# Two transformer blocks on one core: the experts' weights in loads of 2 MB, the last sums onto x, and a branch's loads on another queue

## Chip, core and metric

The kernel runs on one core of a Trainium2 chip. The metric is the device time of one execution in microseconds. PE is the matrix engine, PEld its weight loads, DVE, ACT and POOL (GpSimd) the vector, scalar and general engines, SP the engine whose queue issues nearly all DMAs.

## Reference

256 tokens of width 1024 in float32 go through two blocks. Block 1 has one layer: a mixer (attention over selected keys beside a state-space mixer), then 32 experts of which each token takes 4. Block 2 has two layers of dilated attention beside mLSTM and a convolutional feed-forward part.

```python
def first_block(x, c, ...):
    mod = cond @ w_ada + b_ada
    h = _rms(x, norm_mix) * (1.0 + sc_m) + sh_m
    ...
    x = x + g_m * (mixed @ w_out)
    h = _rms(x, norm_ffn) * (1.0 + sc_f) + sh_f
    x = x + g_f * _moe(h, w_router, b_router, w_gu, b_gu, w_dn, b_dn)

def second_block(x, ...):
    for l in range(2):
        mixed = hybrid_mixer(rms_norm(x, mix_pre_g[l]), w_in[l], ...)
        x = x + rms_norm(mixed, mix_post_g[l])
        ff = conv_ffn(rms_norm(x, ffn_pre_g[l]), w_up[l], ...)
        x = x + rms_norm(ff, ffn_post_g[l])
```

`_moe` takes the top 4 of 32 router values per token, their softmax as gates, and sums `gate * (swiglu(h @ w_gu[e] + b_gu[e]) @ w_dn[e] + b_dn[e])`. `w_gu[e]` is 1024 x 2048 (8 MB), `w_dn[e]` 1024 x 1024 (4 MB).

## The kernel before, in words

All tokens stay in SBUF. The program runs through three stages. The mixer of block 1 ends at about 340 us of the profiled span, the experts at about 1290, and the two layers of block 2 fill the rest.

**The experts.** `moe` gives each expert 64 slots of tokens. `Expert.gate_up(j)` (L1410) takes piece j of `w_gu`, 128 rows of 2048 values: 1 MB, 8 KB a partition. It has four matmul calls, pg and pu (gate and up), each on two halves of the array (64 rows of the output each). `Expert.turn` prepares the way back to tokens, `act` the swiglu (sw_g, sw_t, sw_u) and its transposes (pat), `down` (L1457) multiplies by `w_dn` in four loads of 1 MB into pdn. `out` scales (oe), splits it in two parts (oeH, oeL), and `scatter` (L1487) adds it onto x with two matmuls (pc) and one DVE add for each half of each of two token blocks. In `moe` (L1352) the next expert's piece 0 is multiplied before the expert's `down`, and the sums onto x of an expert stand among the next one's pieces. `in_order` with `TEN` keeps PE's instructions in the written order.

**The ring.** `k.load` puts each weight load into the next of 20 slots of 1 MB (`ring_use`: pools that lie where the mixer's buffers were, in the order `RU`). The loads are on SP's queue; a load is issued when the slot's last reader is done.

**The block past the slots.** Ahead of expert 18, `overflow` (L1506) stands in an `If` (L1512) on the largest count of tokens of an expert. It is not executed with these inputs. Its own loads are on SP's queue too.

**The last expert.** Its sums onto x are also squared on ACT (sq_y) for the next norm (rn_m, rs, then xs on DVE and nf_p, the transposes on PE). `k.warm` puts small matmuls (warm) between, whose result is not used. `OL` sets the order of the norm's steps.

Some lines that matter:

```python
w = k.load([(lambda t: t, self.w_gu[e, j * 128:(j + 1) * 128, :])], [128, 2048])
for n, (p, o) in enumerate(outs):
    nc.tensor.matmul(p[o:o + 64], hg, w[:, n * 512:(n + 1) * 512], ...)
...
with tc.If(go > SLOTS):
```

Of the kernel before, what the change touches and what calls it, by code (L numbers as in the profile page):

```python
# [8 lines left out]
F32 = mybir.dt.float32  # L9
# [4 lines left out]
OP = mybir.AluOpType  # L14
# [12 lines left out]
SD = 1  # L27
OL = 'r0 r1 t00 t01 H00 L00 H01 L01 t10 H10 t11 L10 H11 L11'
# [71 lines left out]
def _pack(a):  # L100
# [13 lines left out]
    for k in ("norm_mix", "b_ada", "norm_ffn", "conv_w", "conv_b", "ssm_norm", "kv_norm"):  # L114
        col(k, a[k])
    col("d_skip", np.repeat(np.asarray(a["d_skip"]).reshape(-1), 64))
# [11 lines left out]
    return {"vec": vec, "row": row.reshape(1, NR)}  # L128

# [16 lines left out]
class K:  # L146
    def __init__(self, tc, i, ctx):
# [13 lines left out]
        self.hold = []  # L161
        self.side = 0
# [53 lines left out]
    def late(self, P):  # L216
# [7 lines left out]
        nc.sync.dma_start(self.wro, i["w_router"][0].rearrange("(k p) e -> p k e", p=128))  # L224
# [79 lines left out]
    def split(self, w, eng=None, into=None):  # L304
# [19 lines left out]
        with ExitStack() as c:  # L324
            for inst in self.hold.pop(0) if self.hold else ():
                c.enter_context(self.tc.issue_after(inst))
            self.splits = [self.nc.scalar.activation(H, w, AF.Copy).ins,  # L327
                           (eng or self.nc.vector).tensor_tensor(L, w, H.bitcast(F32), op=OP.subtract).ins]  # L328
        return H, L
# [159 lines left out]
def ada_end(k, n, s, ones):  # L489

    nc = k.nc
    o = k.ps.tile([128, 512], F32, name="ad_c", tag="tr", bufs=2)
    for j in range(4):
        k.lastc = nc.tensor.matmul(o[:, j:j + 1], s[:, j * 128:(j + 1) * 128], ones, start=True, stop=True)
    kind, half = n // 2, n % 2
# [45 lines left out]
def mixer(k):  # L541
# [185 lines left out]
    def scores(b):  # L727
        S = 128 * (b + 1)
        acc = sm.tile([128, 256], F32, name="acc", bufs=1)[:, :S]
        for g in range(4):  # L730
            h0 = (g // 2) * 4 + g % 2
            pd = ps.tile([128, 2, 256], F32, name="pd", tag="at", bufs=2)
            for u in range(2):
                h = h0 + 2 * u
                o = (h % 2) * 64
                nc.tensor.matmul(pd[:, u, :S], qiT[o:o + 64, h // 2, b * 128:(b + 1) * 128], kiT[o:o + 64, :S],
                                 start=True, stop=True)
            rl = sm.tile([128, 2, 256], F32, name="rl", tag="t2", bufs=3)
            nc.scalar.activation(rl[:, :, :S], pd[:, :, :S], AF.Relu)
            for u in range(2):  # L740
                h = h0 + 2 * u
                if g == 0 and u == 0:
                    nc.vector.tensor_scalar(acc, rl[:, u, :S], wi[:, b, h:h + 1], 0.0, op0=OP.mult, op1=OP.add)
                else:
                    nc.vector.scalar_tensor_tensor(acc, rl[:, u, :S], wi[:, b, h:h + 1], acc,
                                                   op0=OP.mult, op1=OP.add)
# [62 lines left out]
    def attend(q):  # L809
        PT0 = Bp.tile([128, 4, 256], F32, name="PT0", tag="PT0")  # L810
        PT1 = Bp.tile([128, 4, 128], F32, name="PT1", tag="PT1")
        for b in range(NB):
# [3 lines left out]
            for u0 in range(2):  # L816
                pl = ps.tile([128, 2, 256], F32, name="pl", tag="at", bufs=2)
                for u in range(2):
# [3 lines left out]
                                     kT[o:o + 64, h // 2, :S], start=u == 0, stop=False, skip_group_check=True)  # L822
                nc.tensor.matmul(pl[:, :, :S], identr, msk[b][:, None, :].to_broadcast([128, 2, S]),
# [21 lines left out]
        for g in range(2):  # L845
            p = ps.tile([128, 256], F32, name="pv", tag="at", bufs=2)
            for u in range(2):
                hs = slice((4 * q + 2 * g + u) * 64, (4 * q + 2 * g + u) * 64 + 64)
                o = p[u * 64:u * 64 + 64]
                nc.tensor.matmul(o, vv[:, 0, hs], PT0[:, 2 * g + u], start=True, stop=False)  # L850
                nc.tensor.matmul(o[:, 128:], vv[:, 1, hs], PT1[:, 2 * g + u], start=False, stop=True)
# [115 lines left out]
    def quad(q):  # L967
# [17 lines left out]
        for w in range(2):  # L985
            j = 2 * q + w
            p = ps.tile([128, 256], F32, name="py", tag="at", bufs=2)
            for u in range(2):
                h = 2 * j + u
                o = p[u * 64:u * 64 + 64]  # L990
                hs = slice(h * 64, h * 64 + 64)
                nc.tensor.matmul(o, xdt[:, 0, hs], wm[:, 0:2, 2 * w + u], start=True, stop=False)
                nc.tensor.matmul(o[:, 128:], xdt[:, 1, hs], wm[:, 2, 2 * w + u], start=False, stop=True)
# [91 lines left out]
    def turn(b, j0, jn, psum, eng):  # L1085

        p = ps.tile([128, 4, 128], F32, name="xt_p", tag=psum, bufs=2)
        for j in range(jn):
            k.tr(p[:, j], k.x[:, b, (j0 + j) * 128:(j0 + j + 1) * 128])
# [1038 lines left out]
```

## Time and profile before

| | |
|---|---|
| median of 3 runs | 2036.26 us (2033.62 to 2036.63) |
| the profiled execution | 2033.31 us, of which the span is 2031.6 us |
| mean granted clock of PE | 0.975 |
| PE busy | 1889.1 us, 93% of the span |
| DVE, ACT, POOL busy | 1051.6, 746.0, 210.8 us |
| DMA | 583.21 MB in 188091 packets |

Shares of busy time are averages over the three stages. In the experts' stage the DMA rate is level; in the others it is less than half of that. The chain of waits tells which of them a step waits for, and a timeline row's bracket how long its engine was idle before it and what released it.

### The profile page before, as it was taken

The page shows a single profiled execution, that of the slowest core. Times are in us where ns is not written, and L with a number is a line of the kernel's source. Part 1 is how long each engine was busy: PE and PEld are TensorE (multiplying, and loading weights), DVE is VectorE, ACT ScalarE, POOL GpSimd, SP SyncE. Part 2 cuts the span into 40 slices and gives each one's busy share as a digit, 9 for nine tenths or more (in the row PEclk, how much of TensorE's full clock was granted, in tenths as well). Part 3 has the DMA queues.
Part 4 walks back from the last instruction along what each step waited for, and adds up shares of the span by engine and source line. Part 5 has one row for each costly group of instructions (what it writes and reads, how often), then busy time and mean ns, then how long its engine had stood idle before and what let it go on. Part 6 is the DMA issues. An engine that isn't in the chain of part 4 may idle for free.

```text
span 2031.6 us, 28326 instructions
## 1 busy us (share of the span) xinstructions
PE 1889.1 (93%) x11058; PEld 1217.5 (60%) x11059; DVE 1051.6 (52%) x1919; ACT 746.0 (37%) x1477; POOL 210.8 (10%) x378
## 2 busy tenths in 40 slices
PE   6799999999999998869999998898999999989998
PEld 5688887444344433324443333676799877769996
DVE  3788675223222222202222222388689758778984
ACT  4657444111011110101111110355577545556763
POOL 1434310000000000000000000111022111111210
PEclk9899999999999999979999999899999999999999
DMA  9767558999999999999999999633265545325552
GB/s 341 254 224 227 158 201 309 398 420 421 420 420 421 420 420 420 420 374 421 419 420 421 420 420 420 234 131 98 84 208 181 175 149 192 104 83 177 187 177 94
DMA packets 188091, 583.21 MB, mean 287 GB/s; under 512 B 15096, under 2 KB 92424, under 8 KB 138928
## 3 DMA queue, kind: packets, MB, share of 16 engines
q1 hardware_dynamic: 186960, 578.32, 74.3%
q0 software_dynamic: 704, 1.98, 0.4%
q8 instruction: 89, 1.46, 0.3%
q10 hardware_dynamic: 288, 1.05, 0.1%
q14 instruction: 50, 0.41, 0.1%
HBM read 580.23 MB, written 1.07 MB: 286 GB/s over the span
## 4 chain that ended last, share of the span: by engine, by line
PE 37%; DMA 9%; DVE 6%; issue 2%; ACT 1%; POOL 0%; DVEq 0%; POOLq 0%; ACTq 0%; SPq 0%
PE mm L340 8%; PE mm L341 8%; PE mm L339 8%; DMA w<-in_w_gu_dram 6%; DMA w<-in_w_dn_dram 3%; PE pdn L1465 3%; PE pg L1424 3%; PE pu L1424 2%; DVE wL L328 1%; DVE ac L1936 1%; PE apv L1917 1%; ACT wH L327 1%; PE warm L403 0%; PE apl L1895 0%; PE pc L1493 0%
## 5 line engine op out<-in xcount | busy, mean ns | idle before, releaser
L328 DVE TENSOR_TENSOR wL<-w,wH 128x1024 fp32r<-128x1024 f32 (+1 forms) x239 | 307.6, 1288 | 118.3 <-ACT wH L327 115.0
L327 ACT ACTIVATE wH<-w 128x1024 fp32r<-128x1024 f32 (+1 forms) x255 | 267.6, 1052 | 177.0 <-PE mm L340 81.0
L1424 PE MATMUL pg<-w,hg 128*64 128x512 f32 x1024 | 278.2, 616 | 27.4 <-DMA w<-in_w_gu_dram 21.5
L1424 PE MATMUL pu<-w,hg 128*64 128x512 f32 x1024 | 269.0, 597 | 0.0
L1465 PE MATMUL pdn<-w,aT 128*64 128x512 f32 x1024 | 228.4, 595 | 5.9 <-DMA w<-in_w_dn_dram 4.1
L341 PE MATMUL mm<-hnH,wL 128*128 128x256 f32 x800 | 229.1, 286 | 1.2 <-POOL xp L1931 0.8
L339 PE MATMUL mm<-hnH,wH 128*128 128x256 f32 x800 | 226.5, 283 | 0.0
L340 PE MATMUL mm<-hnL,wH 128*128 128x256 f32 x800 | 226.2, 283 | 0.0
L1162 ACT ACTIVATE sw_t<-sw_g 128x512 f32<-128x512 f32 x32 | 20.2, 630 | 466.3 <-DVE sw_g L1161 466.3
L1479 DVE SCALAR_TENSOR_TENSOR oe<-pdn,gs,gf 128x512 f32<-128x512 f32 x32 | 24.0, 751 | 316.6 <-PE pdn L1465 316.6
L1465 PEld LDWEIGHTS pdn<-w,aT 128*64 128x64 f32 x1024 | 72.4, 137 | 156.3 <-issue 122.2
L1424 PEld LDWEIGHTS pu<-w,hg 128*64 128x64 f32 x1024 | 75.3, 138 | 148.2 <-issue 148.2
L341 PEld LDWEIGHTS mm<-hnH,wL 128*128 128x128 f32 x800 | 153.2, 191 | 3.5 <-DVE wL L328 1.3
L339 PEld LDWEIGHTS mm<-hnH,wH 128*128 128x128 f32 x800 | 153.3, 192 | 0.5 <-issue 0.4
L1424 PEld LDWEIGHTS pg<-w,hg 128*64 128x64 f32 x1024 | 60.2, 137 | 155.7 <-issue 77.5
L340 PEld LDWEIGHTS mm<-hnL,wH 128*128 128x128 f32 x800 | 153.3, 192 | 0.0
L1496 DVE TENSOR_TENSOR x<-x,pc 128x512 f32<-128x512 f32 x128 | 82.4, 684 | 122.2 <-PE pc L1494 122.2
L1480 ACT ACTIVATE oeH<-oe 128x512 fp32r<-128x512 f32 x32 | 20.2, 630 | 277.9 <-DVE oe L1479 277.9
L341 PE MATMUL mm<-hH,wL 128*128 128x256 f32 x304 | 91.0, 299 | 11.3 <-DVE wL L328 11.3
L328 POOL TENSOR_TENSOR wHL<-w,wHL 128x1024 fp32r<-128x1024 f32 x1 | 2.4, 2359 | 938.0 <-DMA w<-in_w_in_dram 938.0
L2068 DVE SCALAR_TENSOR_TENSOR fa<-fx,lvec,fa 128x256 f32<-128x256 f32 x176 | 92.7, 527 | 5.1 <-ACT fa L2066 4.3
L339 PE MATMUL mm<-hH,wH 128*128 128x256 f32 x304 | 90.5, 298 | 4.8 <-ACT wH L327 4.3
(551 smaller groups left out, 3426.9 us busy)
## 6 DMA issues: line engine op xcount, KB each, us to landing
w<-in_w_gu_dram SPq DMA_DIRECT2D x256, 1024.0 KB, 19.8
w<-in_w_dn_dram SPq DMA_DIRECT2D x127, 1024.0 KB, 19.8
w<-in_w_in_dram SPq DMA_DIRECT2D x50, 1024.0 KB, 5.6
w<-in_w_up_dram SPq DMA_DIRECT2D x44, 1024.0 KB, 5.1
w<-in_w_down_dram SPq DMA_DIRECT2D x20, 1024.0 KB, 5.0
ad_l<-in_w_ada_dram SPq DMA_DIRECT2D x32, 512.0 KB, 4.3
w<-in_w_out_dram SPq DMA_DIRECT2D x12, 1024.0 KB, 5.1
w<-in_w_ada_dram SPq DMA_DIRECT2D x8, 1024.0 KB, 14.3
```

The costliest lines, as they stand in the source:

```text
L327: self.splits = [self.nc.scalar.activation(H, w, AF.Copy).ins, (eng or self.nc.vector).tensor_tensor(L, w, H.bitcast(F32), op=OP.subtract) ...
L328: (eng or self.nc.vector).tensor_tensor(L, w, H.bitcast(F32), op=OP.subtract).ins]
L339: nc.tensor.matmul(out, sH, mH, start=start, stop=False, **kw)
L340: nc.tensor.matmul(out, sH, mL, start=False, stop=False, **kw)
L341: return nc.tensor.matmul(out, sL, mH, start=False, stop=stop, **kw)
L1424: nc.tensor.matmul(p[o:o + 64], hg, w[:, n * 512:(n + 1) * 512], start=j == 0, stop=j == 7 and e > 0)
L1465: nc.tensor.matmul(pd[c * 64:c * 64 + 64], self.aT[:, j % 4, j // 4], w[:, j - j0, c * 512:(c + 1) * 512], start=j == 0, stop=j == 7)
L1479: nc.vector.scalar_tensor_tensor(oe, self.pd, self.gs, k.gf, op0=OP.mult, op1=OP.mult)
L1496: dx = nc.vector.tensor_tensor(xx, xx, p, op=OP.add)
L1917: nc.tensor.matmul(p[u * 64:u * 64 + 64], vv[:, sb, hs], PT[:, sb, 2 * g + u], start=sb == 0, stop=sb == 1)
L1936: nc.vector.scalar_tensor_tensor(ac, xp[:, q:q + 256], cw[:, q * 8 + j:q * 8 + j + 1], ac, op0=OP.mult, op1=OP.add)
L2068: nc.vector.scalar_tensor_tensor(ac, xp[:, q:q + 256], cw(q, j), ac, op0=OP.mult, op1=OP.add)
```

## The change

1. **Loads.** `w_gu` comes in four loads of 2 MB an expert, `w_dn` in two: a partition reads 16 KB in one run (two rows of `w_gu`, four of `w_dn`). So that the rows match, the features are taken in pairs (`pair(j)`: every second column), the norm's vectors are permuted where the program lays out its inputs, and `act` is transposed by every fourth column. The ring has 10 slots of 2 MB. `TEN` holds SP too, so loads go out in PE's order. The last expert's last pieces come in smaller loads.
2. **The block past the slots** has its loads on GpSimd's queue.
3. **The last sums onto x**: the warm matmuls stand behind all four sums; the four pc have four PSUM buffers; sq_y has another buffer; `behind` keeps the first square after the split of the second weight piece on ACT; `OL` is reordered.
4. **Half-array alternation**: pd, pl, pv, py (mixer of block 1) and apl, apv (block 2) are written so that calls on the two halves of the array take turns.

```diff
-OL = 'r0 r1 t00 t01 H00 L00 H01 L01 t10 H10 t11 L10 H11 L11'
+OL = 'r0 t00 t01 r1 H00 L00 H01 L01 t10 H10 t11 L10 H11 L11'
...
+def pair(j):
+    c = j // 2 * 256 + j % 2
+    return slice(c, c + 255, 2)
...
+    def ring_use(self, order):
+        self.rctx.close()
+        self.shared.close()
+        self.wctx.close()
+        self.big = ExitStack()
+        left, right = (NW + len(self.wz)) // 2, self.nring // 2
+        p = [(self.big.enter_context(self.tc.tile_pool(name=f"big{n}", bufs=1, side="left" if n < left else "right",
+                                                       reuse_waits="tile")), 1) for n in range(left + right)]
+        self.rings, self.nload = [p[n] for n in order], -1
...
-RU = (0,-3,1,2,-1,-2)
+RU = (4,5,3,6,0,1,2,7,8,9)
...
-TEN = (mybir.EngineType.PE,)
+TEN = (mybir.EngineType.PE, mybir.EngineType.SP)
...
-        w = k.load([(lambda t: t, self.w_gu[e, j * 128:(j + 1) * 128, :])], [128, 2048])
+        if j % 2 == 0:
+            src = self.w_gu[e, j * 128:j * 128 + 256, :].rearrange("(p k) c -> p k c", k=2)
+            parts = [slice(0, 1), slice(1, 2)] if self.final and j == 6 else [slice(0, 2)]
+            self.w = k.load([(lambda t, c=c: t[:, c], src[:, c]) for c in parts], [128, 2, 2048])
+        w = self.w[:, j % 2]
...
-            k.tr(pt[:, q].rearrange("p a s -> p (a s)"), act[:, c:c + 255:2])
+            k.tr(pt[:, q].rearrange("p a s -> p (a s)"), act[:, q:q + 509:4])
...
+        for a in range(2):
+            src = self.w_dn[e, a * 512:a * 512 + 512, :].rearrange("(p k) c -> p k c", k=4)
+            parts = [slice(0, 2), slice(2, 3), slice(3, 4)] if self.final and a else [slice(0, 4)]
+            w = k.load([(lambda t, c=c: t[:, c], src[:, c]) for c in parts], [128, 4, 1024])
+            for q in range(4):
                 for c in range(2):
...
+                if E[e].final:
+                    for b in range(NB):
+                        for c in range(2):
+                            k.warm(k.x[:, b, c * 512:c * 512 + 128], WE[3 + 2 * b + c])
...
                 if self.final:
-                    sq = self.M.tile([128, 512], F32, name="sq_y", tag="st", bufs=BST)
+                    sq = self.M.tile([128, 512], F32, name="sq_y", tag="sg", bufs=BSG)
                     aq = nc.scalar.activation(sq, xx, AF.Square, scale=1 / 32, accum_out=k.ssx[:, b, c:c + 1])
-                    k.warm(xx[:, :128], WE[3 + 2 * b + c])
+                    if b + c == 0:
+                        k.behind = aq.ins
...
-                            nc.sync.dma_start(w, w_gu[0, bass.ds(e, 1), j * 128:(j + 1) * 128, c0:c0 + 512]
+                            nc.gpsimd.dma_start(w, w_gu[0, bass.ds(e, 1), pair(j), c0:c0 + 512]
...
-            for u0 in range(2):
-                pl = ps.tile([128, 2, 256], F32, name="apl", tag="at", bufs=2)
-                for u in range(2):
+            pls = [ps.tile([128, 2, 256], F32, name="apl", tag="at", bufs=2) for u0 in range(2)]
+            for u in range(2):
+                for u0, pl in enumerate(pls):
                     h = 4 * q + u0 + 2 * u
                     o = (h % 2) * 64
                     nc.tensor.matmul(pl[:, u], qT[0][o:o + 64, h // 2, b * 128:(b + 1) * 128], qT[1][o:o + 64, h // 2],
                                      start=True, stop=True)
+            for u0, pl in enumerate(pls):
                 nc.vector.tensor_tensor(lg[:, u0:u0 + 3:2], pl, logc[:, b:b + 1].to_broadcast([128, 2, 256]), op=OP.add)
```

How the order of the instructions moves, at three places. First SP's queue where the experts start; a row is the line, the instruction and its tile (cmi is the largest count). Before:

```order
L301 DMA w<-in_w_gu_dram 128x2048 x3
L1301 DMA bgu_r<-in_b_gu_dram 128x512
L1303 DMA bdn<-in_b_dn_dram 32x512 x2
L301 DMA w<-in_w_gu_dram 128x2048 x3
L301 DMA w<-in_w_dn_dram 128x2048 x2
L1511 TENSOR_LOAD cmi
L1511 ISA x2
L301 DMA w<-in_w_dn_dram 128x2048 x2
L301 DMA w<-in_w_gu_dram 128x2048 x8
L301 DMA w<-in_w_dn_dram 128x2048 x4
L301 DMA w<-in_w_gu_dram 128x2048 x8
```

Now:

```order
L323 DMA w<-in_w_gu_dram 128x4096 x2
L1329 DMA bgu_r<-in_b_gu_dram 128x512
L1331 DMA bdn<-in_b_dn_dram 32x512 x2
L323 DMA w<-in_w_gu_dram 128x4096 x2
L1546 TENSOR_LOAD cmi
L1546 ISA x2
L323 DMA w<-in_w_dn_dram 128x4096 x2
L323 DMA w<-in_w_gu_dram 128x4096 x4
L323 DMA w<-in_w_dn_dram 128x4096 x2
L323 DMA w<-in_w_gu_dram 128x4096 x4
L323 DMA w<-in_w_dn_dram 128x4096 x2
L323 DMA w<-in_w_gu_dram 128x4096 x4
```

Loads of 16 KB a partition (4096 values) stand in for two of 8 KB, and expert 1's first piece goes out with its partner ahead of expert 0's `w_dn`, as PE reads it.

Second, SP at the branch ahead of expert 18, with the semaphores that each row waits for: DMAHW are the hardware DMA lanes (loads issued by SP), DMASW the software ones (GpSimd), `sequencer` the engine's own. The last row is the jump past the block. Before:

```order
L301 DMA w<-in_w_gu_dram 128x2048 [waits DMAHW0_49,PE_49]
L301 DMA w<-in_w_gu_dram 128x2048 [waits DMAHW1_49,PE_49]
L301 DMA w<-in_w_gu_dram 128x2048 [waits DMAHW2_49,PE_49]
L1512 COMPARE_AND_BRANCH
L1524 COMPARE_AND_BRANCH
L1524 UNCONDITIONAL_BRANCH [waits SP_sequencer_49,DMAHW0_49,DMAHW1_49,DMAHW2_49,DMAHW3_49,DMAHW4_49,DMAHW5_49,DMAHW6_49,DMAHW7_49]
```

Now:

```order
L323 DMA w<-in_w_dn_dram 128x4096 [waits DMAHW2_49,PE_49]
L323 DMA w<-in_w_dn_dram 128x4096 [waits DMAHW3_49,PE_49]
L323 DMA w<-in_w_gu_dram 128x4096 [waits DMAHW4_49,PE_49]
L1547 COMPARE_AND_BRANCH
L1559 COMPARE_AND_BRANCH
L1559 UNCONDITIONAL_BRANCH [waits SP_sequencer_49]
```

The eight lanes are gone from the jump's waits. On DVE, the first instructions behind the branch, before:

```order
L1417 TENSOR_SCALAR one<-half,pick 128x128 [waits PE_49]
L1161 TENSOR_SCALAR sw_g<-pg 128x512 [waits DMAHW3_49,DMAHW2_49,DMAHW4_49,DMAHW1_49,DMAHW5_49,DMAHW0_49,DMAHW6_49,DVE_49,DMAHW7_49,PE_49,Activation_49]
L1163 TENSOR_SCALAR sw_u<-pu 128x512 [waits DMAHW4_49,DMAHW3_49,DMAHW5_49,DMAHW2_49,DMAHW6_49,DMAHW0_49,DMAHW7_49,DVE_49,PE_49]
L1164 SCALAR_TENSOR_TENSOR sw_u<-sw_u,sw_g 128x512 [waits DVE_49]
L1443 COPY gs<-pgs 128x1 [waits PE_49]
```

Now:

```order
L1448 TENSOR_SCALAR one<-half,pick 128x128 [waits PE_49]
L1189 TENSOR_SCALAR sw_g<-pg 128x512 [waits DMASW3_49,DMASW2_49,DMASW4_49,DMASW1_49,DMASW5_49,DMASW0_49,DMASW6_49,DVE_49,DMASW7_49,PE_49,Activation_49]
L1191 TENSOR_SCALAR sw_u<-pu 128x512 [waits DMASW4_49,DMASW3_49,DMASW5_49,DMASW2_49,DMASW6_49,DMASW1_49,DMASW7_49,DVE_49,PE_49]
L1192 SCALAR_TENSOR_TENSOR sw_u<-sw_u,sw_g 128x512 [waits DVE_49]
L1478 COPY gs<-pgs 128x1 [waits PE_49]
```

The lanes that sw_g and sw_u wait for are now GpSimd's.

Third, PE around the last expert's sums onto x, up to the norm's transposes (nf_p). Before:

```order
L1494 MATMUL pc<-oeL,ST 128x512
L403 MATMUL warm<-x,cst 128x128 x3
L1493 MATMUL pc<-oeH,ST 128x512
L1494 MATMUL pc<-oeL,ST 128x512
L403 MATMUL warm<-x,cst 128x128 x3
L1493 MATMUL pc<-oeH,ST 128x512
L1494 MATMUL pc<-oeL,ST 128x512
L403 MATMUL warm<-x,cst 128x128 x3
L1493 MATMUL pc<-oeH,ST 128x512
L1494 MATMUL pc<-oeL,ST 128x512
L403 MATMUL warm<-x,cst 128x128 x4
L407 MATMUL nf_p<-cst,xs 128x128 x8
```

Now:

```order
L429 MATMUL warm<-oe,cst 128x128 x3
L1527 MATMUL pc<-oeH,ST 128x512
L1528 MATMUL pc<-oeL,ST 128x512
L1527 MATMUL pc<-oeH,ST 128x512
L1528 MATMUL pc<-oeL,ST 128x512
L1527 MATMUL pc<-oeH,ST 128x512
L1528 MATMUL pc<-oeL,ST 128x512
L1527 MATMUL pc<-oeH,ST 128x512
L1528 MATMUL pc<-oeL,ST 128x512
L429 MATMUL warm<-x,cst 128x128 x13
L433 MATMUL nf_p<-cst,xs 128x128 x8
```

The 13 warm matmuls, in four groups between and behind the sums before, stand in one row behind them.

## Rows read from the trace of the kernel before

**Rows 1.** The page: PE's busy time; rate of the DMAs in 40 slices of 50.8 us.
```profile
PE 1889.1 (93%) x11058; PEld 1217.5 (60%) x11059; DVE 1051.6 (52%) x1919; ACT 746.0 (37%) x1477; POOL 210.8 (10%) x378
...
GB/s 341 254 224 227 158 201 309 398 420 421 420 420 421 420 420 420 420 374 421 419 420 421 420 420 420 234 131 98 84 208 181 175 149 192 104 83 177 187 177 94
```

**Rows 2.** The page: packets of all DMA queues by size.
```profile
DMA packets 188091, 583.21 MB, mean 287 GB/s; under 512 B 15096, under 2 KB 92424, under 8 KB 138928
```

**Rows 3.** Windows of 51 us; last: PE's granted clock, DMA share, GB/s.
```profile
561.00:612.00 51.00, 50.67 (x276) 20.64 (x274) 14.82 (x28) 7.14 (x16) 0.00 (x0) 1.00 1.01 420
...
1479.00:1530.00 51.00, 51.00 (x425) 50.91 (x424) 46.93 (x76) 39.47 (x80) 10.94 (x43) 1.00 0.61 196
```

**Rows 4.** Chain of waits, 930 to 1050: start us, us, what.
```profile
931.20 6.87 PE pdn L1465 x32
...
957.52 6.87 PE pdn L1465 x32
```

**Rows 5.** Chain of waits, 1190 to 1260.
```profile
1202.70 19.88 DMA w<-in_w_gu_dram
...
1223.69 0.86 PE pu L1424 x4
```

**Rows 6.** Timeline at the branch: start us, us, what [idle before it, releaser].
```profile
895.98 1.29 SPq L301 DMA_DIRECT2D w<-in_w_gu_dram  x3
896.12 0.69 DVE L1161 TENSOR_SCALAR sw_g<-pg 128x512 f32<-128x512 f32 x1 [16.33 <-SPq L1512]
```

**Rows 7.** The branch's line L1512: ns min/median/max, first and last start us.
```profile
L1512 SPq EVENT_SEMAPHORE  x9: 17/17/17, 881.2 to 895.8; - x9
```

**Rows 8.** Windows of 10 us around the branch, columns as in rows 3.
```profile
880.00:890.00 10.00, 5.64 (x48) 3.43 (x44) 0.00 (x0) 0.00 (x0) 0.00 (x0) 0.89 0.98 404
890.00:900.00 10.00, 0.94 (x4) 0.73 (x4) 2.74 (x5) 2.30 (x6) 0.00 (x0) 0.50 0.52 199
```

**Rows 9.** Windows of 10 us at the experts' start, columns as in rows 3.
```profile
350.00:360.00 10.00, 10.00 (x47) 3.74 (x47) 2.08 (x10) 2.92 (x9) 0.00 (x0) 1.00 0.98 374
...
370.00:380.00 10.00, 9.92 (x53) 4.21 (x54) 0.90 (x3) 1.99 (x5) 0.00 (x0) 1.00 0.91 324
```

**Rows 10.** Timeline of PE: expert 0's last piece, expert 1's piece 1.
```profile
366.52 1.07 PE L1424 MATMUL pu<-w,hg 128*64 128x512 f32 x2
...
380.37 1.03 PE L1424 MATMUL pg<-w,hg 128*64 128x512 f32 x4
381.23 1.03 PE L1424 MATMUL pu<-w,hg 128*64 128x512 f32 x4
```

**Rows 11.** Chain of waits from the last expert into the next norm.
```profile
1280.60 0.70 DVE x L1496
...
1281.35 0.94 PE warm L403 x6
1282.28 0.43 PE pc L1493
...
1287.30 1.65 PE warm L403 x6
...
1294.03 0.76 DVE xs L1601
...
1294.83 1.97 PE nf_p L407 x8
```

**Rows 12.** Timeline there: the last sum and the first square.
```profile
1290.14 0.69 DVE L1496 TENSOR_TENSOR x<-x,pc 128x512 f32<-128x512 f32 x1 [2.89 <-PE pc L1494]
1290.14 0.63 ACT L1499 ACTIVATE sq_y<-x 128x512 f32<-128x512 f32 x1 [8.95 <-PE pc L1494]
```

**Rows 13.** Timeline of PE in the second block: apl and apv.
```profile
1401.54 1.14 PE L1895 MATMUL apl<-aT,aT 64*128 64x256 f32 x8
...
1426.09 1.95 PE L1917 MATMUL apv<-aPT,av 128*64 128x256 f32 x12
...
1429.98 1.13 PE L1895 MATMUL apl<-aT,aT 64*128 64x256 f32 x4
```

More of the change, by code (lines that the diff above doesn't have):

```diff
@@ L161, in __init__ @@
         self.hold = []
+        self.behind = None
         self.side = 0
@@ L328, in split @@
                            (eng or self.nc.vector).tensor_tensor(L, w, H.bitcast(F32), op=OP.subtract).ins]
+        if self.behind and self.npiece == 2:
+            self.tc.add_manual_dep(self.behind, self.splits[0].name, mybir.DependencyInfo(
+                mybir.DependencyClass.NoSync, mybir.DependencyReason.DATA), reason="order")
+            self.behind = None
         return H, L
@@ L492, in ada_end @@
     o = k.ps.tile([128, 512], F32, name="ad_c", tag="tr", bufs=2)
+    kind, half = n // 2, n % 2
     for j in range(4):
-        k.lastc = nc.tensor.matmul(o[:, j:j + 1], s[:, j * 128:(j + 1) * 128], ones, start=True, stop=True)
-    kind, half = n // 2, n % 2
+        c = pair(j) if kind in (3, 4) else slice(j * 128, (j + 1) * 128)
+        k.lastc = nc.tensor.matmul(o[:, j:j + 1], s[:, c], ones, start=True, stop=True)
     cols = slice(half * 4, half * 4 + 4)
@@ L846, in attend @@
             p = ps.tile([128, 256], F32, name="pv", tag="at", bufs=2)
[L847 to L851, printed above, removed]
+            for sb in range(NB):
+                for u in range(2):
+                    hs = slice((4 * q + 2 * g + u) * 64, (4 * q + 2 * g + u) * 64 + 64)
+                    o = p[u * 64:u * 64 + 64, sb * 128:]
+                    nc.tensor.matmul(o, vv[:, sb, hs], (PT1 if sb else PT0)[:, 2 * g + u], start=sb == 0, stop=sb == 1)
             nc.scalar.activation(yH[:, 2 * q + g], p, AF.Copy)
@@ L987, in quad @@
             p = ps.tile([128, 256], F32, name="py", tag="at", bufs=2)
[L988 to L993, printed above, removed]
+            for n in range(2):
+                for u in range(2):
+                    h = 2 * j + u
+                    hs = slice(h * 64, h * 64 + 64)
+                    nc.tensor.matmul(p[u * 64:u * 64 + 64, n * 128:], xdt[:, n, hs],
+                                     wm[:, 2, 2 * w + u] if n else wm[:, 0:2, 2 * w + u], start=n == 0, stop=n == 1)
             yd = sm.tile([128, 256], F32, name="yd", tag="t1", bufs=6)
@@ L1252, in moe @@
     k.anchor = k.after
-    k.ring_use(RU, [n for n in range(len(k.more)) if n not in RU])
+    k.ring_use(RU)
+    ps, sm = k.ps, k.phase(ctx, "smE", 0)
+    M = ctx.enter_context(tc.tile_pool(name="moe", bufs=1, reuse_waits="tile"))
     rs, lg, G, sel, rk, v8 = k.rsx, k.lg, k.G, k.sel, k.rk, k.v8
```

113 lines of the change are left out of this document (56 added, 57 removed).

## The prediction

> **What bounds the kernel now.** I read the slices of the page first. PE is busy for 93% of the span, yet from the ninth slice to the twenty-fifth the DMA rate stands at 420 GB/s with one dip to 374 [rows 1]: these 17 slices are the experts, and whether PE or the stream of weights ends a step there has to be read from the chain. While data is waiting, two pdn groups of successive experts start 957.52 − 931.20 = 26.3 us apart [rows 4]: PE's price of an expert. An expert has 12 MB of weights (12.58 million bytes), which at 420 GB/s (the stretch from 561 [rows 3]) take 30.0 us. So the stream is the slower of the two by 3.6 us an expert. PE lives for a while on what the ring held at the start, and then the chain runs along the loads [rows 5]. What shortens the stream shortens the kernel; what shortens PE's work there is hidden by the stream.
>
> Before the experts (to about 340 us) and behind them (from about 1275 us) the rate is under half of that, and PE and the vector engines set the time. The span is 2031.6 us, its execution 2033.3 us; the median shown, 2036.3 us, is 3 us above it. I make the sum on 2033.3 and add 3 at the end.
>
> **Loads of 2 MB.** 385 loads, nearly all of 1 MB, become 195, five of them smaller than 2 MB. The bytes stay: 384 MB, 384 × 1.0486 = 402.7 MB, 958.7 us at 420 GB/s. What changes is a packet: 8 KB of one partition before (the page counts 188091 packets with 138928 under 8 KB [rows 2]; the 49163 others are the experts' 383 × 128 and a few), 16 KB after. Is a longer packet faster per byte? The trace has no 16 KB packet, so I bound it by two sizes it has. 8 KB: 420 GB/s over 16 engines is 312 ns a packet. 1 KB, in the stretch from 1479, where w_up's pieces are read in rows of 1 KB: 196 GB/s at a busy share of 0.61 [rows 3], so 196 × 1.01 / 0.61 = 325 GB/s at a full share, 50.5 ns a packet. A straight line through both is 37.4 ns a KB and 13.1 ns a packet. Then 16 KB take 611 ns instead of 624: 2.1%, −20 us over the experts. That is one end; the stretch has some smaller packets, so the 13 ns are rather too many. The other end is 0, a rate limited by bytes. The 1 KB row shows that a fixed part exists and 8 KB is the nearer size, so I take three quarters, **−15 us**.
>
> [...]
>
> **The drain at the branch.** Ahead of expert 18 stands a block that is not executed. SP sends nine semaphore events there between 881.2 and 895.8 us [rows 7], and its next loads are issued at 895.98 only; DVE's sw_g waited 16.33 us for it [rows 6]. Why: the block's own loads stand on SP's queue, and the order before shows SP's skip branch waiting for all eight hardware DMA lanes, which are empty only when every load issued has landed. The stream stands meanwhile: 404 and 199 GB/s in two windows of 10 us [rows 8], against 420: 0.4 + 5.3 = 5.6 us of stream lost. [...] In the changed order SP waits for its own sequencer alone, and DVE's sw_g names software lanes, on which GpSimd has long finished. **−5.6 us**; between −3, if the slots at that moment are not free, and −5.6.
>
> **Slots in pairs at the start.** Twenty slots of 1 MB become ten of 2 MB in the same memory: a load now waits until both halves of its slot have been read, and goes out in PE's order. Before, the stream from 350 us lost 1.1 us (374 GB/s) and 2.3 us (324 GB/s) in two windows of 10 us [rows 9]. After, the eleventh load needs the first slot (expert 0, pieces 0 and 1), and the fourteenth the fourth slot, which PE leaves at about 367.6, behind the last pu of expert 0 [rows 10]. The fifteenth needs the slot of expert 1's pieces 0 and 1; PE reads piece 0 before expert 0's pdn, but piece 1 behind it, at 380.37 to 382.26 [rows 10]. The load issued at 367.6 has landed by about 381, so the stream stands about 4 us; two loads for free slots are queued behind that one on SP. The first ten slots also fill later, since those under the mixer's buffers come free in pairs: I reckon some 5 us. What was lost before goes. **+5 us**, from 0 to +8. In steady state seven loads are still on their way while SP waits for such a slot, so nothing stands. SP's queue has nothing else to delay during the experts.
>
> **End of the stream.** The last expert's pieces 4 and 5 come as one load, 5 us ahead of piece 7. PE then has four pieces of 2 × 0.86 us [rows 5] and the bias's matmuls to do, 6.9 us and the bias; 5 of it pass before piece 7 lands, so gate_up ends about 2 us and the bias behind that landing, where it was 1.7: **+1 us** (0 to +2). The last w_dn load is 512 KB, as before.
>
> **The last sums onto x.** Before: pc, x, then three warm matmuls that wait for that x, then the next pc: x starts at 1280.60 and the last of four at 1290.14 [rows 11, 12]; the squares waited 8.95 us on ACT and start only with the last pc [rows 12]; xs starts at 1294.03, nf_p at 1294.83 [rows 11]. After, the four pairs of pc (0.43 us for the first of a pair, some 0.7 a pair) go straight on, four PSUM buffers apart, so the adds of 0.70 run back to back: last x ends at about 1283.4, the first block's squares, rn_m, rs and xs follow by 1285. PE now has 13 warm matmuls in one piece from about 1282.6: at the price of the first group, 0.94 for three, 4.1 us; at that of the later, 1.65 for three, 7.1 us [rows 11]. nf_p then starts between 1286.7 and 1289.7, instead of 1294.83: −8 to −5. The first group came behind busy time and these 13 do too, so **−7.5 us**. The weight pieces for the next matmuls are split on ACT beside it as before; grow is ahead of the first w_in load by half a megabyte, 1.3 us, which the adds hide; uncovered, it would cost that 1.3.
>
> **Alternating halves.** Each part's order of issue is changed in the source; what counts is whether they overlap more. Eight apl passes of two halves, A A B B, take 1.14 us and four of one half 1.13 [rows 13]: where both halves stand side by side they overlap already. In the changed order two fours of apl per layer stay apart from their partners, as before, and the others were together before. So apl gives nothing. apv: 12 passes in 1.95 us [rows 13], against 6 × 0.215 + 0.27 = 1.56 if all were paired (0.86 / 4 = 0.215 is a paired pass of 512 columns [rows 5], so a lone one of 256; the run-out is 1.13 − 4 × 0.215 = 0.27): 0.4 for each of four groups, not all on the path: **−1 us** (0 to −2). The mixer's pd, pl, pv, py: the same sizes, and its order is reshuffled around them: **−1 us** (−4 to +4). Strided columns (pair, every fourth column of act) are in the transposes as every second column was; they cost nothing beside the stream.
>
> **Sum.** −15 − 5.6 + 5 + 1 − 7.5 − 1 − 1 = −24. 2033.3 − 24 = 2009; plus 3: **2012 us**.
>
> **Rivals.**
> 1. *A packet of 16 KB is no faster per byte.* For it: 420 GB/s is held very evenly [rows 1], as if by a limit of bytes; against it, the 1 KB row. The first term falls to 0: −9, 2027 us.
> 2. *Slower.* Longer packets make the stream slower: each packet reads 16 KB from one place in DRAM, and 128 such runs lie 16 KB apart in place of 8. For it: nothing in the trace, which has neither size nor pitch; against it, the bytes of a load are still contiguous as a whole. The price: 1 GB/s less is 402.7 × (1/419 − 1/420) = 2.3 us, so the other terms' −9 are used up at 416 GB/s, 1% down, and 410 GB/s gives +23 − 9 = +14: 2050 us. [...]
> 3. *The warm matmuls eat the tail's gain.* They run at the later price, or nf_p meets a stretch at half the clock: −1.5 in place of −7.5 and the rest the same, 2018 us. For it: the third group before ran at 1.65 [rows 11], and so did the second.
> 4. *The drain stays.* Another wait at the branch holds SP until its lanes are empty: 5.6 us stay: 2018 us. For it: the other engines' branch rows still meet; against it, SP's and DVE's rows.
>
> **Chances.** My forecast 0.46, rival 1 0.25, rival 2 0.09, rival 3 0.12, rival 4 0.08. I count 0.2%, 4 us, as what a measurement of this kernel can tell. Faster by more: the forecast, rivals 3 and all but 0.01 of 4, and 0.20 of rival 1: 0.85. Within: 0.04 of rival 1, 0.01 of 4 and 0.01 of 2: 0.06. Slower: 0.08 of rival 2 and 0.01 of rival 1: 0.09. The range: all terms at their good ends, −20 − 5.6 + 2 − 8 − 2 − 4, is −38, 1998 us; upward it takes in rival 1, with a few us for the start: 1997 to 2028.
>
> **What would show it.** The rate in the experts' windows: about 427 GB/s is my value, 420 rival 1, under 416 rival 2; the mean issue-to-landing time of a load roughly doubles whatever happens. No hole near the branch, and no idle DVE before sw_g there. A hole of about 4 us in the stream near 380 us. From the last pdn to nf_p some 10 us in place of 17. The layers behind the experts as long as before within 2 us. I am wrong if the mixer's order moves the router's result by more than 5 us, or if PE, not the loads, ends the experts' steps.

## The result and the profile after

The changed kernel takes 2011.11 us (median of 4 runs, 2010.1 to 2011.91) against 2035.80 before: a ratio of 0.988, 95% interval 0.9863 to 0.9897, 24.7 us less. The forecast was 2012. The two profiled executions took 2033.31 and 2011.91 us, and their spans differ by 21.3 us. One of r6's eleven runs, 2138.0 us at a mean granted clock of 0.839, was in a slower state and is left out.

The page of the changed kernel: busy time, the rate in 40 slices, the packets, and the two groups of weight loads (last number: median us from issue to landing).

```profile
PE 1878.5 (93%) x11058; PEld 1218.2 (61%) x11059; DVE 1049.3 (52%) x1919; ACT 746.4 (37%) x1477; POOL 216.3 (11%) x378
...
GB/s 339 247 220 200 183 204 275 385 427 427 426 427 427 427 428 427 427 425 428 427 427 427 427 427 424 246 135 84 118 197 180 188 150 164 105 94 173 185 178 95
DMA packets 160216, 583.17 MB, mean 290 GB/s; under 512 B 11544, under 2 KB 88872, under 8 KB 135376
...
w<-in_w_gu_dram SPq DMA_DIRECT2D x127, 2048.0 KB, 33.7
w<-in_w_dn_dram SPq DMA_DIRECT2D x63, 2048.0 KB, 39.1
```

The level in the experts' slices is 427 instead of 420 [rows 1], the dip to 374 is gone, and a load is on its way for 34 to 39 us. Two windows of 51 us, in the middle of the experts and around the branch (last columns: granted clock, DMA share, GB/s):

```profile
561.00:612.00 51.00, 50.77 (x278) 20.65 (x276) 14.55 (x27) 7.16 (x16) 0.00 (x0) 1.00 1.01 428
...
867.00:918.00 51.00, 50.77 (x270) 20.93 (x268) 10.82 (x22) 6.47 (x15) 0.00 (x0) 0.98 1.01 427
```

These answer to [rows 3] and [rows 8]: no hole. Behind the branch sw_g waits for PE alone, 2.51 us in place of 16.33 for SP [rows 6]:

```profile
881.26 0.69 DVE L1189 TENSOR_SCALAR sw_g<-pg 128x512 f32<-128x512 f32 x1 [2.51 <-PE pg L1459]
```

PE itself still stands for 6.2 us at its own branch, but the stream goes on, and from 923 us the chain of waits runs along the loads again. The start, in windows of 10 us, answers to [rows 9]:

```profile
350.00:360.00 10.00, 10.00 (x48) 3.52 (x46) 1.97 (x8) 0.98 (x3) 0.00 (x0) 1.00 1.00 397
...
370.00:380.00 10.00, 10.00 (x51) 3.54 (x51) 0.70 (x1) 1.99 (x5) 0.00 (x0) 1.00 0.84 351
380.00:390.00 10.00, 10.00 (x48) 3.10 (x44) 3.32 (x6) 0.63 (x1) 0.00 (x0) 1.00 0.80 311
```

At 420 to 427 the three would be full; (427 − 397 + 427 − 351 + 427 − 311) / 427 × 10 us = 5.2 us are missing, where [rows 9] miss 3.4. Then the chain of waits through the last expert (start us, us, what):

```profile
1199.37 39.12 DMA w<-in_w_dn_dram
1238.53 3.65 PE pdn L1499 x16
1242.18 0.86 PE pg L1459 x4
...
1255.79 0.86 PE pu L1459 x4
...
1267.60 0.76 DVE oe L1513
```

Up to 1238.53 the chain is the loads; from there PE runs without a wait for data. The last oe starts at 1267.60; before it was 1277.82, 10.2 us later. The mixer has a part in this. Its last matmuls, the transposes for the router (xt_p), before and in the changed kernel (ns min/median/max, first and last start us):

```profile
L407 PE MATMUL xt_p<-cst,x x16: 270/272/308, 327.5 to 340.4; 128*128 128x128 f32 x16
```

```profile
L433 PE MATMUL xt_p<-cst,x x16: 270/283/357, 325.4 to 338.4; 128*128 128x128 f32 x16
```

The mixer ended 2.0 us sooner, so the experts gave 8.3. Last, the timeline of the sums (bracket: idle before it, releaser):

```profile
1270.38 2.48 DVE L1530 TENSOR_TENSOR x<-x,pc 128x512 f32<-128x512 f32 x4 [0.59 <-PE pc L1528]
...
1271.12 3.17 PE L429 MATMUL warm<-x,cst 128*128 128x128 f32 x26
1271.15 0.63 ACT L1533 ACTIVATE sq_y<-x 128x512 f32<-128x512 f32 x1 [0.18 <-ACT wHL L349]
...
1273.64 1.42 DVE L1636 SCALAR_TENSOR_TENSOR xs<-x,rs,grow 128x512 f32<-128x512 f32 x2
...
1274.44 1.32 PE L433 MATMUL nf_p<-cst,xs 128*128 128x128 f32 x8 [0.16 <-DVE xs L1636]
```

The four adds are one row of 2.48 us, the 13 warm matmuls (26 passes) one of 3.17 us, and nf_p starts 6.8 us after oe began. Before, it was 17.0 (oe at 1277.82, nf_p at 1294.83 [rows 11]). So the tail gave 10.2 us too. What is left of the span's 21.3 us, 0.9, lies in the layers behind.

### The profile page after: what moved, and what is told of

Same layout as the page of the kernel before. It is cut to its first block, busy times and chain, and to the rows that moved or that the text cites. A ratio compares the mean times of both kernels' runs of the same rounds, so it can differ in the third digit from the quotient of the medians.

```text
span 2010.3 us, 27892 instructions
## 1 busy us (share of the span) xinstructions
PE 1878.5 (93%) x11058; PEld 1218.2 (61%) x11059; DVE 1049.3 (52%) x1919; ACT 746.4 (37%) x1477; POOL 216.3 (11%) x378
## 4 chain that ended last, share of the span: by engine, by line
PE 33%; DMA 15%; DVE 5%; issue 2%; ACT 2%; POOL 0%; SPq 0%; DVEq 0%; POOLq 0%; ACTq 0%
DMA w<-in_w_gu_dram 9%; PE mm L366 8%; PE mm L367 8%; PE mm L365 8%; DMA w<-in_w_dn_dram 6%; PE pdn L1499 2%; PE pg L1459 1%; PE pu L1459 1%; DVE wL L350 1%; DVE ac L1975 1%; PE apl L1933 1%; ACT wH L349 1%; PE po L2017 0%; PE apv L1956 0%; DVE x L1709 0%
## 5 line engine op out<-in xcount | busy, mean ns | idle before, releaser
L350 DVE TENSOR_TENSOR wL<-w,wH 128x1024 fp32r<-128x1024 f32 (+1 forms) x239 | 302.8, 1268 | 118.8 <-ACT wH L349 112.4
L1459 PEld LDWEIGHTS pg<-w,hg 128*64 128x64 f32 x1024 | 64.6, 137 | 126.3 <-issue 106.2
L350 POOL TENSOR_TENSOR wHL<-w,wHL 128x1024 fp32r<-128x1024 f32 x1 | 2.4, 2402 | 929.7 <-DMA cst<-in_cst_dram 929.7
```

## The experiments

Each kernel was timed in rounds beside the kernel before, on the same chip. The kernel before had medians of 2034.4 us (r1 to r8) and 2032.8 (r9 to r11) there; its own runs spread over some 9 us.

Whole times hide a part of what an edit does, because the mixer ends up to 4 us apart in traces of the same mixer code. What follows it repeats closely: from the last xt_p to the last oe the kernel before takes 937.41 us, and r5, whose edit comes later, 937.42; two traces of the changed kernel take 929.15 and 929.22. So each edit is also read from the stretch that it touches (us, one trace each; r3, at half the rate, left out):

| kernel | last xt_p starts | from there to the last oe | from nf_p to the end |
|---|---|---|---|
| before | 340.4 | 937.4 | 736.7 |
| changed | 338.4 | 929.2 | 735.8 |
| changed again (r11) | 336.6 | 929.2 | 735.6 |
| r1 | 335.4 | 932.3 | 736.4 |
| r2 | 336.0 | 941.7 | 735.7 |
| r4 | 342.3 | 929.4 | 738.0 |
| r5 | 342.1 | 937.4 | 737.0 |
| r6 | 341.1 | 934.0 | 736.8 |
| r7 | 337.6 | 929.5 | 736.5 |
| r8 | 339.4 | 924.4 | 733.7 |
| r9 | 336.2 | 924.4 | 733.7 |
| r10 | 337.3 | 929.7 | 735.3 |

From the last oe to nf_p it is 17.0 us in the kernel before and in r6, and 6.8 to 6.9 in the others.

**r1: the branch's loads back on SP.**

```diff
-                            nc.gpsimd.dma_start(w, w_gu[...])
+                            nc.sync.dma_start(w, w_gu[...])
```

and the same for the block's three other loads.

> The changed kernel with one part undone: the loads of the block past the slots stand on SP's queue again, so SP's jump past the block waits for its DMA lanes. My theory (the forecast's term): the stream stands while the lanes run empty, two windows of 10 us show about 404 and 200 GB/s again, and the time is 5 to 6 us above the changed kernel, 2016 to 2017 us. Rival: the pause lets the sixteen DMA engines line up again, which in the changed kernel drift apart (the last of a load's sixteen parts lands about 8 us behind the first near the end of the experts), and part of the 5.6 us comes back as loads that land sooner behind the branch: the hole is there, but the time is only 2 to 3.5 us above, 2013 to 2014.5 us.

2012.5 us (2011.8 to 2012.78): 1.4 above the changed kernel. The hole is there. Windows of 10 us:

```profile
870.00:880.00 10.00, 10.00 (x59) 3.86 (x56) 0.29 (x1) 0.00 (x0) 0.00 (x0) 1.00 0.98 416
880.00:890.00 10.00, 3.88 (x22) 2.87 (x24) 2.74 (x5) 2.90 (x7) 0.00 (x0) 0.83 0.60 214
```

(427 − 416 + 427 − 214) / 427 × 10 = 5.2 us of stream. Yet the whole time rises by 1.4 only. One reason is the mixer, which ended 3.0 us sooner in r1's trace than in the changed kernel's; from there to the last oe r1 takes 3.1 us more. That still leaves 2.1 of the 5.2. The trace has every DMA engine's mark that it is done with its part of a load, sixteen for each load. From the first to the last of the sixteen it takes, median over the loads that land in a stretch, in us:

```
landing at        before   changed   r1 (drain back)   r6 (drain gone)
400 to 500 us       3.2       1.8          1.8               2.9
800 to 860 us       6.3       4.9          5.1               5.4
910 to 1000 us      1.9       6.4          2.1               6.8
1200 to 1240 us     3.5       8.1          3.4               9.1
```

PE waits for the last of the sixteen: in the changed kernel the last mark of expert 30's second `w_dn` load is at 1238.48 us, and its pdn starts at 1238.53. The sixteen drift apart there as the stream goes on, from 1.8 to 8.1 us. A pause puts them in line again: behind it they are 1.9 us apart in the kernel before and 2.1 in r1, without it 6.4 and, in r6, 6.8. In the last stretch the last mark is 4.0 us behind the sixteen's mean in the changed kernel, 1.9 in r1. Counted from the last xt_p, the second `w_dn` load of expert 30 lands at 896.1 us in the mean of its marks in the changed kernel and at 901.3 in r1, 5.2 later; its last mark lands at 900.0 and 903.2, 3.2 later. So the stream loses the whole hole, and PE sees some 3 us of it. The rival's mechanism holds, at the size that it gave.

**r6: part 2 alone, on the kernel before.** The same edit the other way.

```diff
-                            nc.sync.dma_start(w, w_gu[...])
+                            nc.gpsimd.dma_start(w, w_gu[...])
```

> The kernel before with part 2 alone (the loads of the block past the slots on GpSimd's queue). First theory: the whole hole of 5.6 us goes, 5 to 6 us below the kernel before. Rival, borne out by the run with part 2 undone: the pause also lined up the sixteen DMA engines, so without it the last loads of the experts land later against the mean of the stream, and only 1 to 3.5 us are left.

2031.4 us (2027.8 to 2034.2, ten runs), ratio 0.9983 (0.9973 to 0.9992): 1.6 to 5.5 us below, middle 3.5 by the ratio, 3.1 by the medians. Windows of 10 us:

```profile
880.00:890.00 10.00, 10.00 (x70) 5.33 (x68) 2.83 (x5) 2.90 (x7) 0.00 (x0) 1.00 1.01 419
890.00:900.00 10.00, 10.00 (x50) 3.32 (x48) 2.47 (x4) 0.63 (x1) 0.00 (x0) 1.00 1.01 420
```

Against [rows 8] the hole is closed, and the drift goes on to 9.1 us. From the last xt_p to the last oe it takes 3.5 us less than the kernel before: the last gate and up piece lands 6.0 us sooner in the mean of its marks, 3.4 sooner by the last one. Both runs speak against a gain of 5.6.

**r2: 8 KB packets in the slots of 2 MB.**

```diff
-            parts = [slice(0, 1), slice(1, 2)] if self.final and j == 6 else [slice(0, 2)]
+            parts = [slice(0, 1), slice(1, 2)]
```

and the same for `w_dn` (two loads of two rows of a partition).

> The changed kernel with the same ten slots of 2 MB, but each 2 MB slot is filled by two loads of 1 MB that each take 8 KB a partition (every second row of the pair), so packets are 8 KB as before. My theory, the packet: the rate in the experts' windows falls from 427 back to 420 GB/s, and the time rises by 13 to 16 us, 2024 to 2027 us. Rival, the size or the number of loads, or the kernel's order: the rate stays at 427 and the time within 3 us of 2011.

2022.11 us (2021.91 to 2024.9): 11 above.

```profile
561.00:612.00 51.00, 50.77 (x262) 19.85 (x262) 13.07 (x26) 6.21 (x14) 0.00 (x0) 1.00 1.01 420
```

420 again, with everything else of the change in place. Its mixer happened to end 2.4 us sooner and its finer pieces shorten the last expert, so a little is given back. From the last xt_p to the last oe it takes 12.5 us more than the changed kernel. Packet or load? The next two runs keep the packet at 16 KB and halve the load.

**r3: two loads over 64 partitions each.**

```diff
-            self.w = k.load([(lambda t, c=c: t[:, c], src[:, c]) for c in parts], [128, 2, 2048])
+            hs = (slice(0, 64), slice(64, 128)) if len(parts) == 1 else (slice(0, 128),)
+            self.w = k.load([(lambda t, c=c, h=h: t[h, c], src[h, c]) for c in parts for h in hs], [128, 2, 2048])
```

and the same for `w_dn`.

> The changed kernel, each 2 MB load split into two of 1 MB over 64 partitions each: packets stay 16 KB, loads are half as large and twice as many, and the eight lanes hold 8 MB on the way instead of up to 16. If the packet decides: 427 GB/s and 2009 to 2013 us; and if the sixteen DMA engines drift apart because so much is on the way, the last loads land sooner and it is 2 to 4 us faster. If the size of a load decides: 420 GB/s and 2024 to 2027 us.

2639.84 us (2561.58 to 2707.68), so that even the fastest run is 550 us above the changed kernel. Neither expectation: the rate halved.

```profile
561.00:612.00 51.00, 31.09 (x128) 11.68 (x126) 7.45 (x13) 3.57 (x8) 0.00 (x0) 0.80 1.00 220
```

All sixteen engines are busy (share 1.00), but a 16 KB packet takes 1125 ns (median) in place of 614. The trace does not tell what the packets of a half load wait for.

**r10: the same with every second partition.**

```diff
-            hs = (slice(0, 64), slice(64, 128)) if len(parts) == 1 else (slice(0, 128),)
+            hs = (slice(0, 128, 2), slice(1, 128, 2)) if len(parts) == 1 else (slice(0, 128),)
```

against r3, and the same for `w_dn`.

> Like the run with loads over 64 partitions (215 GB/s, 16 KB packets at 1125 ns in place of 614), but each half load takes every second partition instead of the lower or upper 64. [...] If it is slow because each of the sixteen DMA engines has only four packets of a load: about 215 GB/s and 2560 to 2710 us.

2010.88 us (2009.23 to 2012.25).

```profile
561.00:612.00 51.00, 50.77 (x277) 20.66 (x274) 14.14 (x27) 7.06 (x16) 0.00 (x0) 1.00 1.01 426
```

426 GB/s, 614 ns a packet: half loads of 1 MB with 16 KB packets are as fast as loads of 2 MB. They have 64 packets for the sixteen engines, as r3's have, so that number is not what makes r3 slow. So the packet decides the rate, and r3's loss came from which partitions its half loads take: 220 GB/s over the lower and the upper 64, 426 over the even and the odd ones. Why that matters no run here shows. The two also read DRAM differently, r3 1 MB in a row and r10 every second 16 KB; but the kernel before reads 1 MB in a row too, at 420 GB/s, which speaks against that side as the cause.

**r4: part 4 undone.** pd, pl, pv, py, apl and apv have the order of calls of the kernel before; of apv:

```diff
-            for sb in range(NB):
-                for u in range(2):
-                    hs = slice((4 * q + 2 * g + u) * 64, (4 * q + 2 * g + u) * 64 + 64)
+            for u in range(2):
+                hs = slice((4 * q + 2 * g + u) * 64, (4 * q + 2 * g + u) * 64 + 64)
+                for sb in range(NB):
```

> The changed kernel with the order of calls in pd, pl, pv, py, apl and apv as before (part 4 undone). My theory: alternation gave 1 us in the block 2 layers and 1 to 2 in the mixer, so 2012 to 2014 us. Rival: it gave nothing, or the mixer's reshuffled order only moved work about: 2010 to 2012 us.

2018.2 us (2013.48 to 2020.34), ratio 0.9916 (0.99 to 0.9932) against 0.988 and, in r11, 0.9893: 7.1 us by the medians, 5 to 7 by the ratios, more than both theories. Where? The mixer's end (xt_p) in r4 and in r11:

```profile
L433 PE MATMUL xt_p<-cst,x x16: 270/283/357, 329.3 to 342.3; 128*128 128x128 f32 x16
```

```profile
L433 PE MATMUL xt_p<-cst,x x16: 270/283/357, 323.6 to 336.6; 128*128 128x128 f32 x16
```

With alternation the last xt_p starts between 335.4 and 339.4 in eight traces (mean 337.1; r3, whose slow loads run beside the mixer from 200 us on, has 340.9 and is left out), without it between 340.4 and 342.3 in four (mean 341.5; the kernel before, r4, r5, r6). So part 4 gave about 4 us there. From nf_p to the end the kernels without it take 736.7 to 738.0 us (mean 737.1), those with it 733.7 to 736.5 (mean 735.3): 1.8 us in the layers, 1.4 without r8 and r9.

**r11: the changed kernel again.**

> The changed kernel itself once more, on the same chip as the two others. For my reading of part 4 (2018.2 us without it, 2013.5 to 2020.3) the changed kernel has to stay at 2010 to 2012.5 us and its mixer (last router transposes at 338.5 us in its first trace, 342.3 without part 4) within 2 us of that. If its mixer moves by 3 us or more from run to run with the same code, then most of what the mixer showed there is spread, and only the 2 us behind the experts are part 4's.

2011.09 us (2009.91 to 2012.51); its mixer ended 1.9 us sooner than in the first trace, under the 3 us that were set as the limit. Over the eight traces with alternation it moves by 4.0, though, as much as r4's distance from the changed kernel. So no single pair shows part 4's gain in the mixer; the two groups of traces do, whose ranges do not meet when r3 is left out.

**r5: part 3 alone, on the kernel before.**

```diff
-OL = 'r0 r1 t00 t01 H00 L00 H01 L01 t10 H10 t11 L10 H11 L11'
+OL = 'r0 t00 t01 r1 H00 L00 H01 L01 t10 H10 t11 L10 H11 L11'
...
-                    sq = self.M.tile([128, 512], F32, name="sq_y", tag="st", bufs=BST)
+                    sq = self.M.tile([128, 512], F32, name="sq_y", tag="sg", bufs=BSG)
...
-                    k.warm(xx[:, :128], WE[3 + 2 * b + c])
+                    if b + c == 0:
+                        k.behind = aq.ins
```

with the warm matmuls in one loop behind the sums, and the holds of two of the norm's steps to match. The four PSUM buffers of pc, listed with part 3, the kernel before has too, so they are no part of the gain.

> The kernel before with part 3 alone (last sums onto x, squares, warm matmuls behind, order of the norm). My theory after the trace of the changed kernel, where the path from the last oe to nf_p took 6.8 us in place of 17.0: 10 to 11 us below the kernel before. Rival, that part of those 10 us came with the earlier weight loads of the changed kernel: 5 to 8 us below.

2025.14 us (2024.37 to 2025.87), 9.3 below. The last oe in its chain:

```profile
1279.52 0.76 DVE oe L1488
```

Its nf_p starts at 1286.37, 6.9 us later (6.8 in the changed kernel). The tail's gain is its own and needs none of the other parts.

**r7: without the 13 warm matmuls.**

```diff
-                            k.warm(k.x[:, b, c * 512:c * 512 + 128], WE[3 + 2 * b + c])
+                            pass
```

> The changed kernel without the 13 warm matmuls behind the last sums (their result is not used). In the changed kernel nf_p waits for xs, not for them, so if they only fill time, nothing changes: 2009 to 2012 us. Rival: they hold the granted clock, PE idles some 3 us without them, and the first matmuls of the next layer run at the lower level (0.43 us apart in place of 0.23, as in the kernel before): 2 to 6 us slower.

2013.21 us (2010.62 to 2016.11). nf_p starts 6.8 us after oe's start, as with them. The window from 1270, first without them, then in the changed kernel:

```profile
1270.00:1280.00 10.00, 5.78 (x21) 4.10 (x18) 8.86 (x16) 6.68 (x15) 7.38 (x9) 0.71 0.36 116
```

```profile
1270.00:1280.00 10.00, 8.75 (x54) 6.61 (x54) 8.68 (x15) 7.23 (x16) 7.74 (x9) 1.00 0.37 122
```

The granted clock falls to 0.71 in the mean without them, and the first matmul of the next layer takes 0.79 us in place of 0.50; the span is the same (2010.4 and 2010.3), with a mixer that ended 0.9 us sooner. The clock is theirs. From nf_p to the end r7 takes 736.5 us, the changed kernel 735.8 and 735.6; whether that is their worth, or the 2 us of the medians, or nothing, four runs and one trace don't tell.

**r8: pieces 0 and 1 of the next expert ahead of down.**

```diff
-                E[e + 1].gate_up(0, hgs[(e + 1) // 2][:, 0, (1 - u) * SLOTS:(2 - u) * SLOTS])
+                for j in range(2):
+                    E[e + 1].gate_up(j, hgs[(e + 1) // 2][:, j, (1 - u) * SLOTS:(2 - u) * SLOTS])
```

> The changed kernel with the next expert's pieces 0 and 1 both ahead of an expert's down (before: piece 0 alone). The slot that both share is then free 8 us sooner. My theory: the hole of about 3 to 4 us in the stream near 380 us goes, and after the last down's second load PE has one piece less to do, 1.7 us: 3.5 to 5.5 us below the changed kernel, 2005.5 to 2007.5 us. Rival: the stream's loss at the start comes from the slots under the mixer's buffers, and the end is bound by the last pieces: within 1.5 us of 2011.

2005.82 us (2003.46 to 2007.12): 5.3 below the changed kernel. The two windows that missed 4.5 us:

```profile
370.00:380.00 10.00, 10.00 (x54) 4.28 (x54) 0.55 (x1) 1.99 (x5) 0.00 (x0) 1.00 1.01 427
380.00:390.00 10.00, 9.84 (x46) 3.19 (x44) 4.01 (x6) 0.63 (x1) 0.00 (x0) 1.00 1.00 424
```

They are full. From the last xt_p to the last oe r8 takes 924.4 us, 4.8 less than the changed kernel, as the theory had it. It is also 2 us shorter from nf_p to the end, and so is r9, where no line was changed; why was not tried. The end of its chain:

```profile
1200.78 39.11 DMA w<-in_w_gu_dram
...
1239.94 1.08 PE pg L1460 x4
...
1252.05 0.86 PE pu L1460 x4
...
1263.86 0.76 DVE oe L1514
```

The wait that ends last has moved on from the second `w_dn` load of expert 30 to pieces 2 and 3 of expert 31, at 1239.94. PE again has work without a wait from there.

**r9: r8, and the last expert's pairs in two loads each.**

```diff
-            parts = [slice(0, 1), slice(1, 2)] if self.final and j == 6 else [slice(0, 2)]
+            parts = [slice(0, 1), slice(1, 2)] if self.final and j else [slice(0, 2)]
```

> The kernel with pieces 0 and 1 early, and the last expert's pairs of gate and up pieces behind the first each in two loads of 1 MB. In the trace with pieces 0 and 1 early PE runs without a wait from the last expert's piece 2 on, which came with piece 3 at 1239.9: it can start one half load sooner. My theory: 1 to 1.5 us less, 2004.3 to 2004.8 us. Rival: PE is bound by the slowest of the sixteen DMA engines, some 8 us apart, and half loads land hardly sooner: within 0.5 us of 2005.8.

2003.03 us (2002.34 to 2004.22), ratio 0.9852 (0.9835 to 0.9869): faster than both kernels, 8 us below the changed one on the same chip (r11). It is 2.8 less than r8, but the trace gives the split no part in that: from the last xt_p to the last oe both take 924.4 us, and the mixer ended 3.2 us sooner in r9's trace. PE's waits for data in the last expert are gone from its timeline, which has this instead:

```profile
1224.92 1.88 PE L1460 MATMUL pu<-w,hg 128*64 128x512 f32 x4
1226.58 1.92 PE L1460 MATMUL pg<-w,hg 128*64 128x512 f32 x4
```

Two groups take nearly twice their usual 1.03 us; the granted clock is 0.58 in the mean from 1225 to 1229. Whether the split would gain something at the full clock is open.

## Why the prediction came out right, and where its terms were off

The forecast was −24 and the medians show −24.7, but several terms were off and cancelled, so that the hit within 1 us is partly luck. The forecast also set its −24 against the profiled execution and put 3 us on top for the median; between the profiled executions the change is 21.4.

- **Packets, −15.** Right. The rate came out at 427 as forecast; 402.7 × (1/420 − 1/427) = −15.7 us, and r2 takes 11 of it back, 12.5 from the mixer's end, with finer pieces at the end as its advantage. r10 excludes the load's size. Rivals 1 and 2 fall. The straight line through the 1 KB and 8 KB rows gave 611 ns for 16 KB, the trace 614: the packet's fixed part is there, somewhat smaller than the line made it (12 ns by the medians of 313 and 614, the line 13.1). The three quarters that the forecast took of the line's −20 were a choice; that it fits is luck.
- **The drain, −5.6.** The mechanism on SP held (rival 4 falls), the size did not: −3.5 (r6), and 3.1 to put it back (r1), both from the mixer's end to the last oe. The step that failed is that a pause costs only the stream it loses. It also lines up the sixteen engines (1.9 us apart behind it in the kernel before, 2.1 in r1), and 2.0 to 2.6 us came back that way. r1 and r6 show the drift with and without the pause; why the engines drift was not tried.
- **Slots in pairs, +5.** By the packets in the trace 33 MB (loads of 1 MB) had landed at 395.6 us in place of 389.6. The mixer ended 2.0 us sooner, so counted from its end it is +7.9, the upper end of the forecast's range. The hole at 380 came where the order said, and r8, which frees that slot earlier, closes it: it has the 33 MB 4.4 us sooner after its mixer's end.
- **End of the stream, +1.** The size held, the place was wrong. The forecast goes by pieces 4 and 5; the chain shows that the wait that ends last is the second `w_dn` load of expert 30. From its landing PE has 18.1 us to the end of gate_up (1238.53 to 1256.65), while the 6 MB that follow need 14.7 us. So the experts end PE-bound, 3.4 us behind the last of them; the kernel before ended 2.0 behind its last piece (landed at 1264.88, gate_up done at 1266.86). That is +1.4. In r8 gate_up ends 3.1 us behind the last piece and in r9 2.7, so most of r8's 4.8 comes from the start.
- **The last sums, −7.5.** −10.2 in the trace; r5 alone has 6.85 us there too and is 9.3 below in the median. The path was the one described. What was mis-sized is the warm matmuls: 3.17 us for 26 passes, 0.122 each, where the forecast took 0.94 / 6 = 0.157 as the lower end; by the two rows, of 6 and of 26, a pass is 0.11 us and a group's run-out 0.27, which the short group's price holds. nf_p then waits for xs, not for them, and r7, without them, starts it no sooner. Rival 3 falls.
- **Alternation, −1 and −1.** About −4 in the mixer and −1.4 to −1.8 in the layers, by the means of the traces with and without it; −2.0 and −0.9 in the two traces before and after. The forecast had read apl from pairs that overlap already, and gave the mixer's order no sign; it has one. Which of pd, pl, pv, py it comes from was not tried.

In the two traces the terms are: mixer −2.0; start +7.9; packets −14.4 behind the 33 MB (the rest of the −15.7 lies ahead of them); hole −5.6; drift +2.0; end +1.4; last sums −10.2; layers −0.9. They make −21.8, and the spans differ by 21.3. The medians' further 3.3 lie in the executions: the profiled one was 2.5 us below its median before and 0.8 above it after.

Three readings of the prediction were wrong, though its sum hardly hangs on them. Before the experts the rate isn't under half of 420 GB/s: [rows 1] have 341 to 158, most of them above 210. The trace before does have packets of 16 KB, 89 on an instruction queue, with a median of 1072 ns; the weights' packets of that size take 614, so they would have misled. And the lower end of the range has a +2 where the stated good ends of the start and of the end of the stream are 0; with these it is −39.6, which still gives about the 1997 that was stated.

## What to carry to other kernels

Price a change of a packet's size by a line through the packet sizes that the trace has, but take the line as an upper end: here it was right to 0.5% of a packet and gave −20 us where −15.7 came. When loads become larger, look for the last wait anew, at both ends: which slot is held by a half-read pair, and how much work stands behind the last load that is waited for; moving one matmul piece across a step was worth 4.8 us in the experts. A removed pause in a stream wasn't worth its length here, 3.1 to 3.5 us for a hole of 5.2 to 5.6, so undo it on the chip before counting it. And read an edit's worth from the stretch of the trace that it touches: here the mixer ahead moved the whole time by up to 4 us, so that 3.1 us looked like 1.4 and no gain like 2.8.

## What the runs showed of the hardware

- The sixteen DMA engines that share each load drift apart: between the first and the last mark from 1.8 to 8.1 us over 800 us of stream in the changed kernel (loads of 2 MB), from 2.9 to 9.1 in r6 (1 MB). A pause of some 5 us brings them back to 1.9 in the kernel before and 2.1 in r1. The rate row doesn't show it: it stays at 427 in the changed kernel.
- Two loads over the lower and the upper 64 partitions halve the rate (r3: 220 GB/s in the window above) with all engines busy (share 1.00); over even and odd partitions they don't (r10: 426).
- 16 KB a partition in one run gives 427 GB/s, 8 KB 420, one core alone; for 1 KB the prediction's estimate from [rows 3] is 325 at a full share. The packets' medians are 614 and 313 ns: 8 KB more take 301 ns, which leaves 12 ns of each that don't grow with its size.
